# P4's accumulating loads issued behind P7's, and parked slabs moved in pieces, in a two-layer encoder trunk

## The chip, the cores and the metric

The kernel runs on one core of one Trainium2 chip. The metric is the device time of one execution in microseconds (us); lower is better. Three executions of the kernel before gave 1471.56, 1477.7 and 1478.32 us, median 1477.7 us.

## The reference

Two layers of one mixer over 512 positions of width 2048, all in float32, batch 1. Each layer normalises, projects once to all parts, runs three head groups side by side, gates, projects back, normalises and adds to the residual:

```python
for l in range(DEPTH):                       # DEPTH = 2
    h = rmsnorm(x, pre_norm_g[l])
    z = h @ w_in[l]                          # one combined projection
    q_lat, kv_lat, k_pe, gb, gc, xin, q_mem, gate = split_cols(z)
    ...                                      # group A: latent attention, 8 heads, rotary key
    a_out = mla_attention(q, k, v)           # softmax over all 512 positions
    c_out = short_gated_conv(gb, gc, xin, conv_w[l])               # group B: gb * conv3(gc * xin)
    m_out = memory_attention(q_mem, rmsnorm(mem, ...), w_mk[l], w_mv[l])   # group C: 256 memory tokens
    y = jnp.concatenate([a_out, c_out, m_out], axis=-1) * jax.nn.silu(gate)
    x = x + rmsnorm(y @ w_o[l], post_norm_g[l])
```

## The kernel before

**Products.** A float32 product is made of three matmuls on parts with few mantissa bits (`fp32r`): each operand is a high half and a low half, and TensorE adds high x high, high x low and low x high (L272 to L274). The weights' halves are made on the chip from a loaded tile `wr`: ScalarE casts it to `wh` (L189), and VectorE subtracts `wh` from `wr` to get `wl` (L190). This is done two units ahead of TensorE, in pools of three buffers; raw tiles are loaded some six units further ahead, in a pool of eight.

**Groups.** The input projection is cut into groups of two blocks of 512 columns each (416 in group gs[2]). A group is computed with seven products P1 to P7 in place of eight, in Winograd's form of Strassen's scheme, whose right operands are sums of the four weight blocks B11, B12, B21, B22. Each product has four parts c = 0..3, and one part is one step: 12 matmuls on TensorE. The output projection is cut in the same way.

**Where the sums of weights come from.** In a group of the kind `STEADY` (gs[2], gs[3] and gs[4] of each layer, six in all) the order of products is P1; P5 and P2 by turns; P6 and P3 by turns; P7; P4. One tile T per part c begins as B11 for P1. For P5, VectorE adds B12 to it, and for P6, B22 (L178), both loaded by SP. For P4, B21 is added by the transfer itself: a load with `accum_op` add, issued by POOL (the function `more`, L146). P3 uses B22 as loaded; P7 uses the same tile after an accumulating load of B12, also from POOL. An accumulating load can be issued only when the halves of the tile's use before have been made: P4's part c after P6's, P7's part c after P3's. As P6 and P3 go by turns, so do P4's and P7's loads in POOL's queue, though TensorE needs all of P7 before any of P4. A unit's `behind` holds its accumulating load back until the unit it names has been prepared: in groups of the kind `SECOND` (most of the output projection) parts 2 and 3 of P4 wait so for P7's last part.

**Parked slabs.** Results of the projection that are needed in another layout (gc and gb of the convolution, query latents ql, key and value latents kvl, the memory queries qm, the gates gm, ga0, ga1) are written by POOL to DRAM (`sent`, L945: one transfer of 1 MB, kvl in two) and later fetched back into a slab in SBUF with the positions in another order (`fetched`, L952: four transfers of 256 KB, by b = 0..3). A list of calls between the steps says where: gc and gb are written at steps 7 and 8 of gs[2] and fetched at step 3 of gs[3], ql and kvl written at step 21 of gs[3] and fetched at step 2 of gs[4] (tiles cqL, ckvL), qm and gm written at steps 5 and 6 of gs[4], qm fetched at step 10 (QmL), gm at step 23. Then come Km, the rotary table `tab` and Vm, which are read in the mixer behind the group.

**Order.** TensorE, POOL and SP run their instructions in the order in which the code writes them. Beyond the opening part of the kernel VectorE and ScalarE run in an order that a scheduler chose at build time. POOL's transfers complete on eight lanes in turn, and one waits until the transfer eight before it has landed.

Of the kernel before, what the change touches and what calls it, by code (L numbers as in the profile page):

```python
# [5 lines left out]
F32 = mybir.dt.float32  # L6
# [6 lines left out]
P = 128  # L13
D = 2048
# [213 lines left out]
def encoder(tc, x, xt, mem, memt, positions, columns, w_in, q_norm_g, w_uq, w_qr, kv_norm_g, w_ukv,  # L228
# [22 lines left out]
    G = {}  # L251
# [245 lines left out]
    def group(left, key, w, block, slot, passes, final, hold=None, by_two=False, direct=None):  # L497
# [25 lines left out]
        def unit(q, c):  # L523
            k = lambda n: (key, n, c)

            def of(name, loads=(), more=None, sums=(), then=(), **kw):
                at = {"B11": (0, 0), "B12": (0, 1), "B21": (1, 0), "B22": (1, 1)}
                return Unit(k(name), {k(to): [block(*at[n], c)] for to, n in loads}, more and block(*at[more], c),
                            [(k(a), k(b)) for a, b in sums], [(k(a), k(b)) for a, b in then], **kw)
# [5 lines left out]
            if q == "P4":  # L535
                return of("T", more="B21", alloc=hold, behind=(key, "B22", 3) if passes is SECOND and c > 1 else None)
# [401 lines left out]
    def sent(key, *parts):  # L938

        n = sum(t.shape[-1] for t in parts) // 4  # L940
        d = G["sent", key] = dram.tile([4, P, n], F32, name=nm(f"sent{key}"))
        o = 0
        for t in parts:
            w = t.shape[-1] // 4
            nc.gpsimd.dma_start(d[:, :, o:o + w].rearrange("b q k -> q b k"), t.rearrange("q (b k) -> q b k", b=4))  # L945
            o += w

    def fetched(key, name, c=4):

        t, d = slab(name), G.pop(("sent", key))  # L950
        for b in range(4):
            nc.gpsimd.dma_start(t[32 * b:32 * b + 32, :512 * c].rearrange("i (p k) -> i p k", p=4),  # L952
                              d[b].rearrange("(p i) k -> i p k", p=4))
        return t

    def sent_rows(name, C):
        def f():
            pr.until(lambda: C.get((name, "turned")) == NT)
            sent(name, C[name, "slab"])
        return f  # L960

    def gate_back(k, name):
        def f():
            G["ys"][k] = spots(fetched(name, "y"))
        return f

    def conv_back():
        G["uw"] = fetched("gc", "u")
        G["ys"][2] = spots(fetched("gb", "y"))
# [65 lines left out]
    def latents_sent(l):  # L1035
        pr.until(lambda: G.get("normalised") == l)
        sent("ql", G.pop("ql"))
        kv = G.pop("kvl")
        sent("kvl", kv[:, :1024], kv[:, 1024:1536])

    def latents_back():
        G["cqw"], G["ckw"] = fetched("ql", "cqL"), fetched("kvl", "ckvL", 3)
# [242 lines left out]
    def mixer(l, C, pair2, tail):  # L1285
# [5 lines left out]
        add(sent_rows("ga1", C))  # L1291
# [10 lines left out]
        between.setdefault(2, []).append((sent_rows("ga0", C), []))  # L1302
        between.setdefault(11, []).append((gate_back(0, "ga0"), []))
# [3 lines left out]
        between.setdefault(18, []).append((gate_back(1, "ga1"), []))  # L1307
# [165 lines left out]

    def weave(steps, extra, every, n=1):

        out, extra = [], list(extra)
        for k, s in enumerate(steps):
            out.append(s)
            if (k + 1) % every == 0:
                out += extra[:n]  # L1480
                extra = extra[n:]
        return out + extra
# [10 lines left out]
    for l in range(depth):  # L1493
# [109 lines left out]
        put(*gs[l > 0][2:])  # L1603
        add(owns[2])
        steps = [s for passes in gs[2] for s in passes]
        put(steps[:7])
        add(sent_rows(("gb", "gc")[l], C))
        put(steps[7:8])
        add(sent_rows(("gc", "gb")[l], C))
        if l == 0:  # L1610
            add(tables)
        put(steps[8:])
        add(owns[3])
        add(lambda l=l: latents_rows(l))
        steps = [s for passes in gs[3] for s in passes]
        put(steps[:2])
        add(lambda l=l, C=C: latents_begin(l, C))
        put(steps[2:3])
        add(conv_back)
        put(steps[3:8])  # L1620
        add(lambda l=l, C=C: k_rope(l, C))
        put(steps[8:18])
        add(lambda l=l: pr.until(lambda: G.get("normalised") == l))
        put(steps[18:21])
        add(lambda l=l: latents_sent(l))
        put(steps[21:22])
        add(conv(l, 0))
        put(steps[22:25])
        add(conv(l, 1))
        put(steps[25:])  # L1630
        add(owns[4])
        g4 = [s for steps in gs[4] for s in steps]
        put(g4[:1])
        add(conv(l, 2))
        put(g4[1:2])
        add(latents_back)
        put(g4[2:3])
        add(conv(l, 3))
        put(g4[3:5])
        add(sent_rows("qm", C))  # L1640
        put(g4[5:6])
        add(sent_rows("gm", C))
        if l == 0:
            add(tables_wide)
        put(g4[6:7])
        add(latents_parts)
        put(g4[7:9])
        if l == 0:
            add(tables_turned)
        put(g4[9:10])  # L1650
        add(lambda: G.update(qmw=fetched("qm", "QmL")))
        put(g4[10:20])
        add(qm_parts)
        put(g4[20:23])
        add(gate_back(3, "gm"))
        put(g4[23:26])
        add(mem_fetch("Km", 4))
        put(g4[26:27])
        add(tables_fetch)
        put(g4[27:])  # L1660
# [92 lines left out]
```

## Time and profile before

| what | value |
|---|---|
| median of three executions | 1477.7 us (1471.56 to 1478.32) |
| the profiled execution | 1476.04 us, its span 1474.3 us |
| TensorE (PE) busy | 1442.1 us, 98% of the span |
| VectorE (DVE) / ScalarE (ACT) / GpSimd (POOL) busy | 1138.1 / 868.7 / 288.6 us |
| mean granted TensorE clock | 0.994 |
| moved by POOL's queue (q0, software) / SP's (q1, hardware) | 146.03 MB / 162.35 MB |
| accumulating loads of `w_in`, 512 KB: issue to landing | 92, median 7.3 us |
| plain loads of `w_in`, 512 KB, by SP: issue to landing | 128, median 5.8 us |

The profile is of one execution. Times inside it count from the start of the span. A row of waits names the engine and line that waited, for whom, and the total, the count and the longest in us. A row of the timeline gives start and length in us, engine, line, operation, the tile written and the tile read, and in brackets how long the engine stood idle before and who released it. A row of transfers gives what is written and read, the issuing engine, how many, the size of each and the median time from issue to landing. In a row of a group of instructions the busy time and the mean length of one (ns) stand behind the first bar. The "clock" is the share of TensorE's full clock that was granted.

### The profile page before, as it was taken

The numbers are of one execution on the slowest core, as the hardware profiler recorded it, in microseconds if no ns is written. First come the engines' busy times: TensorE is split into PE (matmuls) and PEld (weight loads), VectorE is DVE, ScalarE is ACT, GpSimd is POOL, SyncE is SP. The second block draws the span as 40 slices with busy tenths as digits, with TensorE's granted clock in tenths as the row PEclk, the third lists the DMA queues.
The fourth block names the chain that finished last, engine by engine and source line by source line (L and its number), as shares of the span: only waits on it lengthen the run. The fifth ranks groups of instructions, "written<-read, shape, count | busy, mean of one in ns | idle before, by whom it ended". The sixth has DMA issues, their size and how long they took to land.

```text
span 1474.3 us, 19214 instructions
## 1 busy us (share of the span) xinstructions
PE 1442.1 (98%) x6944; PEld 1223.7 (83%) x6944; DVE 1138.1 (77%) x1517; ACT 868.7 (59%) x1330; POOL 288.6 (20%) x330
## 2 busy tenths in 40 slices
PE   9999999999899999999999999999989999999997
PEld 8887889887688888888898888898867888888886
DVE  5899688696667789769788765768957787688687
ACT  7856344564457788754687433446554586786443
POOL 0032302232132010220220233022322120003111
PEclk9999999999999999999999999999999999999999
DMA  9999977789599194595987999788997984138973
GB/s 358 404 273 211 222 218 143 209 181 314 147 253 265 52 266 133 111 193 172 340 304 224 235 211 226 225 170 219 192 296 162 313 213 97 47 86 151 262 173 128
DMA packets 145567, 309.61 MB, mean 210 GB/s; under 512 B 11008, under 2 KB 32000, under 8 KB 141632
## 3 DMA queue, kind: packets, MB, share of 16 engines
q0 software_dynamic: 58720, 146.03, 45.5%
q1 hardware_dynamic: 86752, 162.35, 34.5%
q8 instruction: 54, 0.88, 0.3%
q14 instruction: 41, 0.34, 0.1%
HBM read 270.47 MB, written 37.88 MB: 209 GB/s over the span
## 4 chain that ended last, share of the span: by engine, by line
PE 71%; DMA 10%; DVE 8%; issue 8%; ACT 2%; POOL 1%; POOLq 0%; SPq 0%; DVEq 0%; ACTq 0%
PE P L273 16%; PE P L274 16%; PE P L272 15%; DMA wr<-in_w_in_dram 7%; DVE wl L190 4%; PE ptp L1219 2%; PE o L273 1%; PE o L274 1%; PE o L272 1%; PE sc L274 1%; PE sc L273 1%; PE sc L272 1%; ACT wh L189 1%; PE qps L272 1%; POOL wr L146 1%
## 5 line engine op out<-in xcount | busy, mean ns | idle before, releaser
L189 ACT CAST wh<-wr 128x1024 fp32r<-128x1024 f32 (+2 forms) x436 | 443.7, 1023 | 437.2 <-PE P L274 306.4
L190 DVE TENSOR_TENSOR wl<-wr,wh 128x1024 fp32r<-128x1024 f32 (+2 forms) x436 | 513.2, 1183 | 198.0 <-ACT wh L189 195.0
L273 PE MATMUL P<-wl,S 128*128 128x512 f32 (+1 forms) x896 | 345.9, 386 | 9.7 <-DVE wl L190 9.5
L272 PE MATMUL P<-wh,S 128*128 128x512 f32 (+1 forms) x896 | 344.9, 385 | 1.9 <-ACT wh L189 1.9
L274 PE MATMUL P<-wh,S 128*128 128x512 f32 (+1 forms) x896 | 344.3, 384 | 0.0
L273 PE MATMUL P<-wl,A 128*128 128x512 f32 (+1 forms) x656 | 253.9, 387 | 10.3 <-DVE wl L190 10.3
L272 PE MATMUL P<-wh,A 128*128 128x512 f32 (+1 forms) x656 | 253.5, 386 | 0.0
L274 PE MATMUL P<-wh,A 128*128 128x512 f32 (+1 forms) x656 | 252.3, 385 | 0.0
L273 PEld LDWEIGHTS P<-wl,S 128*128 128x128 f32 x896 | 168.8, 188 | 43.3 <-DVE wl L190 13.2
L272 PEld LDWEIGHTS P<-wh,S 128*128 128x128 f32 x896 | 168.6, 188 | 32.6 <-ACT wh L189 2.2
L274 PEld LDWEIGHTS P<-wh,S 128*128 128x128 f32 x896 | 168.9, 189 | 30.2
L146 POOL DMA_DIRECT2D wr<-in_w_in_dram x108 | 130.8, 1211 | 305.5 <-DVE wl L190 194.4
L273 PEld LDWEIGHTS P<-wl,A 128*128 128x128 f32 x656 | 123.8, 189 | 36.3 <-DVE wl L190 14.7
L272 PEld LDWEIGHTS P<-wh,A 128*128 128x128 f32 x656 | 123.8, 189 | 22.1 <-ACT og L592 0.2
L274 PEld LDWEIGHTS P<-wh,A 128*128 128x128 f32 x656 | 123.7, 189 | 22.0
L146 POOL DMA_DIRECT2D wr<-in_w_o_dram x40 | 48.8, 1295 | 298.7 <-DVE wl L190 292.8
L178 DVE TENSOR_TENSOR wr<-wr,wr 128x1024 f32<-128x1024 f32 (+1 forms) x60 | 70.0, 1168 | 44.4 <-DMA wr<-in_w_in_dram 43.8
L1206 ACT ACTIVATE P<-sc,nm 128x512 f32<-128x512 f32 (+1 forms) x96 | 59.9, 625 | 28.8 <-DVE nm L1203 28.8
L1209 ACT ACTIVATE P<-P,rec 128x512 f32<-128x512 f32 (+1 forms) x96 | 62.6, 663 | 6.2 <-DVE rec L1208 6.2
L1203 DVE TENSOR_REDUCE nm<-sc 128x1 f32<-128x512 f32 (+1 forms) x96 | 56.4, 594 | 9.1 <-PE sc L1201 8.0
L1219 PE MATMUL ptp<-identr,P 128*128 128x128 f32 x320 | 46.1, 272 | 0.3 <-ACT P L1209 0.3
L1219 PEld LDWEIGHTS ptp<-identr,P 128*128 128x128 f32 x320 | 38.2, 140 | 6.5 <-ACT P L1209 0.7
(325 smaller groups left out, 2102.3 us busy)
## 6 DMA issues: line engine op xcount, KB each, us to landing
wr<-in_w_in_dram SPq DMA_DIRECT2D x128, 512.0 KB, 5.8
wr<-in_w_in_dram POOLq DMA_DIRECT2D x92, 512.0 KB, 7.3
wr<-in_w_o_dram SPq DMA_DIRECT2D x48, 512.0 KB, 6.8
wr<-in_w_o_dram POOLq DMA_DIRECT2D x40, 512.0 KB, 6.7
wr<-in_w_in_dram SPq DMA_DIRECT2D x32, 416.0 KB, 3.9
wr<-in_w_mk_dram SPq DMA_DIRECT2D x15, 512.0 KB, 8.7
wr<-in_w_mv_dram SPq DMA_DIRECT2D x15, 512.0 KB, 10.6
wr<-in_w_in_dram POOLq DMA_DIRECT2D x16, 416.0 KB, 6.7
```

The source lines that it names most:

```text
L146: engine.dma_start(dst, src, **kw)
L178: nc.vector.tensor_tensor(tiles[a], tiles[a], tiles[b], op=ALU.add)
L189: pin(nc.scalar.copy(hi[:, h], src[:, h]))
L190: pin(nc.vector.tensor_tensor(lo[:, h], src[:, h], hi[:, h].bitcast(F32), op=ALU.subtract))
L272: nc.tensor.matmul(ps, ah, bh, start=first, stop=False, **kw)
L273: nc.tensor.matmul(ps, ah, bl, start=False, stop=False, **kw)
L274: nc.tensor.matmul(ps, al, bh, start=False, stop=last, **kw)
L1203: nc.vector.tensor_reduce(nmax, ps, axis=AX.X, op=ALU.max, negate=True)
L1206: nc.scalar.activation(pt, ps, AF.Exp, bias=nmax, accum_out=tot)
L1209: nc.scalar.activation(pt, pt, AF.Copy, scale=rec)
L1219: nc.tensor.transpose(ps[:, k * P:(k + 1) * P], pt[:, k * P:(k + 1) * P], G["ident"])
```

## The change

In `STEADY` groups P4's part c now waits behind a use of B22's part (c + 3) mod 4: part 0 behind P3's part 3, parts 1 to 3 behind P7's parts 0 to 2. And `sent` and `fetched` return lists of four pieces of 256 KB each (kvl is still written in two), which a new function `beside_steps` puts one by one ahead of consecutive steps. New places: in gs[2] steps 4 to 7 and 8 to 11 for the convolution's rows; in gs[3] steps 0 to 3 and 4 to 7 for their fetches and 20 to 25 for ql and kvl; in gs[4] steps 0 to 7 for the latents' fetch (their split moves from step 6 to 9), 4 to 7 and 8 to 11 for qm and gm, 18 to 21 for the fetch of QmL (10 before; its split from 20 to 22) and 23 to 26 for gm's. In the mixer ga1 is written in four pieces at once, ga0 in four pieces between places 2 and 5, and both are fetched piece by piece from 10 and 18 on.

```diff
             if q == "P4":
-                return of("T", more="B21", alloc=hold, behind=(key, "B22", 3) if passes is SECOND and c > 1 else None)
+                return of("T", more="B21", alloc=hold, behind=(key, "B22", 3) if passes is SECOND and c > 1 else
+                          (key, "B22", (c + 3) % 4) if passes is STEADY else None)
...
-    def sent(key, *parts):
-
-        n = sum(t.shape[-1] for t in parts) // 4
-        d = G["sent", key] = dram.tile([4, P, n], F32, name=nm(f"sent{key}"))
-        o = 0
-        for t in parts:
-            w = t.shape[-1] // 4
-            nc.gpsimd.dma_start(d[:, :, o:o + w].rearrange("b q k -> q b k"), t.rearrange("q (b k) -> q b k", b=4))
-            o += w
-
-    def fetched(key, name, c=4):
-
-        t, d = slab(name), G.pop(("sent", key))
-        for b in range(4):
-            nc.gpsimd.dma_start(t[32 * b:32 * b + 32, :512 * c].rearrange("i (p k) -> i p k", p=4),
-                              d[b].rearrange("(p i) k -> i p k", p=4))
-        return t
+    def sent(key, source, *widths):
+
+        def piece(n, b):
+            def f():
+                t, o = source(), sum(widths[:n])
+                if (n, b) in ((0, 0), (0, None)):
+                    G["sent", key] = dram.tile([4, P, sum(widths) // 4], F32, name=nm(f"sent{key}"))
+                w = widths[n] // 4
+                d, t = G["sent", key][:, :, o // 4:o // 4 + w], t[:, o:o + widths[n]].rearrange("q (b k) -> q b k", b=4)
+                if b is None:
+                    nc.gpsimd.dma_start(d.rearrange("b q k -> q b k"), t)
+                else:
+                    nc.gpsimd.dma_start(d[b], t[:, b])
+            return f
+        if len(widths) > 1:
+            return [piece(n, None) for n in range(len(widths))]
+        return [piece(0, b) for b in range(4)]
+
+    def fetched(key, name, there, c=4):
+
+        def piece(b):
+            def f():
+                if b == 0:
+                    G["back", key] = slab(name)
+                t, d = G["back", key], G["sent", key]
+                nc.gpsimd.dma_start(t[32 * b:32 * b + 32, :512 * c].rearrange("i (p k) -> i p k", p=4),
+                                    d[b].rearrange("(p i) k -> i p k", p=4))
+                if b == 3:
+                    there(G.pop(("back", key)))
+            return f
+        return [piece(b) for b in range(4)]
...
-        between.setdefault(2, []).append((sent_rows("ga0", C), []))
-        between.setdefault(11, []).append((gate_back(0, "ga0"), []))
+        for k, f in zip((2, 3, 4, 5), rows_sent("ga0", C)):
+            between.setdefault(k, []).append((f, []))
+        for k, f in zip((10, 11, 12, 13), y_back(0, "ga0")):
+            between.setdefault(k, []).append((f, []))
...
+    def beside_steps(steps, extra):
+        at = {}
+        for first, fs in extra:
+            for k, f in enumerate(fs):
+                at.setdefault(first + k, []).append(f)
+        for k in range(max([len(steps)] + [n + 1 for n in at])):
+            for f in at.get(k, ()):
+                add(f)
+            put(steps[k:k + 1])
...
-        put(steps[:2])
-        add(lambda l=l, C=C: latents_begin(l, C))
-        put(steps[2:3])
-        add(conv_back)
...
-        put(steps[18:21])
-        add(lambda l=l: latents_sent(l))
...
+        beside_steps([s for passes in gs[3] for s in passes],
+                     [(0, fetched("gc", "u", kept_as("uw"))), (2, [lambda l=l, C=C: latents_begin(l, C)]),
+                      (4, y_back(2, "gb")), (8, [lambda l=l, C=C: k_rope(l, C)]),
+                      (18, [lambda l=l: pr.until(lambda: G.get("normalised") == l)]),
+                      (20, latents_sent(l)), (21, [conv(l, 0)]), (25, [conv(l, 1)])])
...
-        put(g4[9:10])
-        add(lambda: G.update(qmw=fetched("qm", "QmL")))
-        put(g4[10:20])
-        add(qm_parts)
...
+        beside_steps([s for passes in gs[4] for s in passes],
+                     [(0, latents_back()), (1, [conv(l, 2)]), (3, [conv(l, 3)]), (4, rows_sent("qm", C)), (6, wide),
+                      (8, rows_sent("gm", C)), (8, turned), (9, [latents_parts]), (18, fetched("qm", "QmL", kept_as("qmw"))),
+                      (22, [qm_parts]), (23, y_back(3, "gm")), (26, [mem_fetch("Km", 4)]), (27, [tables_fetch])])
```

How POOL's queue moves is seen in three places of layer 0. In these rows `wr_` with its number is a weight tile, and each row an accumulating load into it or a transfer to or from a parked slab; the line of the fetch is L952 before and L964 now, of the write L945 before and L949 or L951 now.

The end of gs[2], before (tiles 1682, 1702, 1720 and 1738 are T's parts 0 to 3, loaded for P4; the others are P7's):

```order
L146 DMA wr_1682<-in_w_in_dram 128x2x416
L146 DMA wr_1917<-in_w_in_dram 128x2x416
L146 DMA wr_1702<-in_w_in_dram 128x2x416
L146 DMA wr_1956<-in_w_in_dram 128x2x416
L146 DMA wr_1720<-in_w_in_dram 128x2x416
L146 DMA wr_2010<-in_w_in_dram 128x2x416
L146 DMA wr_1738<-in_w_in_dram 128x2x416
L146 DMA wr_2051<-in_w_in_dram 128x2x416
```

And now:

```order
L146 DMA wr_1919<-in_w_in_dram 128x2x416
L146 DMA wr_1960<-in_w_in_dram 128x2x416
L146 DMA wr_1998<-in_w_in_dram 128x2x416
L146 DMA wr_2056<-in_w_in_dram 128x2x416
L146 DMA wr_1682<-in_w_in_dram 128x2x416
L146 DMA wr_1702<-in_w_in_dram 128x2x416
L146 DMA wr_1720<-in_w_in_dram 128x2x416
L146 DMA wr_1738<-in_w_in_dram 128x2x416
```

P7's four parts now stand in a row, and P4's behind them.

The seam of gs[3] and gs[4], before (2275 to 2329 are P4's tiles):

```order
L146 DMA wr_2329<-in_w_in_dram 128x2x512
L146 DMA wr_2676<-in_w_in_dram 128x2x512
L945 DMA sentql_2884<-ql_2469 128x4x512
L945 DMA sentkvl_2886<-kvl_2470 128x4x256
L945 DMA sentkvl_2886<-kvl_2470 128x4x128
L952 DMA cqL_3088<-sentql_2884 32x4x512 x4
L952 DMA ckvL_3093<-sentkvl_2886 32x4x384 x4
L945 DMA sentqm_3165<-qm_2426 128x4x512
```

And now:

```order
L146 DMA wr_2682<-in_w_in_dram 128x2x512
L146 DMA wr_2280<-in_w_in_dram 128x2x512
L146 DMA wr_2299<-in_w_in_dram 128x2x512
L146 DMA wr_2317<-in_w_in_dram 128x2x512
L951 DMA sentql_2871<-ql_2479 128x512
L146 DMA wr_2335<-in_w_in_dram 128x2x512
L951 DMA sentql_2871<-ql_2479 128x512 x3
L949 DMA sentkvl_2962<-kvl_2480 128x4x256
L949 DMA sentkvl_2962<-kvl_2480 128x4x128
L964 DMA cqL_3052<-sentql_2871 32x4x512 x4
L964 DMA ckvL_3148<-sentkvl_2962 32x4x384
L951 DMA sentqm_3150<-qm_2432 128x512
```

P4's four loads stand behind P7's (the first row is P7's part 3), one piece of ql between them and the other pieces behind; the fetch of ckvL (row by row) is mixed with the pieces of qm.

The end of gs[4], before (2866 to 2932 are P4's tiles; QmL's four pieces are one row):

```order
L952 DMA QmL_3288<-sentqm_3165 32x4x512 x4
L146 DMA wr_2866<-in_w_in_dram 128x2x512
L146 DMA wr_3144<-in_w_in_dram 128x2x512
L146 DMA wr_2889<-in_w_in_dram 128x2x512
L146 DMA wr_3191<-in_w_in_dram 128x2x512
L146 DMA wr_2914<-in_w_in_dram 128x2x512
L146 DMA wr_3234<-in_w_in_dram 128x2x512
L146 DMA wr_2932<-in_w_in_dram 128x2x512
L146 DMA wr_3293<-in_w_in_dram 128x2x512
L952 DMA y_3545<-sentgm_3185 32x4x512 x4
```

And now (P4's tiles are 2873 to 2938):

```order
L146 DMA wr_3300<-in_w_in_dram 128x2x512
L146 DMA wr_2873<-in_w_in_dram 128x2x512
L964 DMA QmL_3452<-sentqm_3150 32x4x512
L146 DMA wr_2900<-in_w_in_dram 128x2x512
L964 DMA QmL_3452<-sentqm_3150 32x4x512
L146 DMA wr_2919<-in_w_in_dram 128x2x512
L964 DMA QmL_3452<-sentqm_3150 32x4x512
L146 DMA wr_2938<-in_w_in_dram 128x2x512
L964 DMA QmL_3452<-sentqm_3150 32x4x512
L964 DMA y_3560<-sentgm_3236 32x4x512 x4
```

QmL's fetch has moved from ahead of all eight loads to between P4's four.

More of the change, by code (lines that the diff above doesn't have):

```diff
@@ L956, in sent_rows @@
-    def sent_rows(name, C):
-        def f():
-            pr.until(lambda: C.get((name, "turned")) == NT)
[L959 to L969, printed above, removed]
+    def sent(key, source, *widths):
[14 more added lines that the diff above has]
+        return [piece(0, b) for b in range(4)]
@@ L971, in conv, with rows_sent, source, kept_as @@
+    def rows_sent(name, C):
+        def source():
+            pr.until(lambda: C.get((name, "turned")) == NT)
+            return C[name, "slab"]
+        return sent(name, source, D)
+    def kept_as(name):
+        return lambda t: G.update({name: t})
+    def y_back(k, name):
+        return fetched(name, "y", lambda t: G["ys"].update({k: spots(t)}))
     def conv(l, c):
@@ L1035, in latents_sent, with source, f @@
     def latents_sent(l):
[L1036 to L1039, printed above, removed]
+        def source(name):
+            def f():
+                pr.until(lambda: G.get("normalised") == l)
+                return G[name]
+            return f
+        return sent("ql", source("ql"), D) + sent("kvl", source("kvl"), 1024, 512)
     def latents_back():
-        G["cqw"], G["ckw"] = fetched("ql", "cqL"), fetched("kvl", "ckvL", 3)
+        return fetched("ql", "cqL", kept_as("cqw")) + fetched("kvl", "ckvL", kept_as("ckw"), 3)
     def latents_parts():
@@ L1290, in mixer @@
         put(p0[1:])
-        add(sent_rows("ga1", C))
+        for f in rows_sent("ga1", C):
+            add(f)
         add(lambda: nc.scalar.activation(small(1, "ex"), C["ga0"][:, NT - 1][:, 0, :1], AF.Exp, scale=0.0))
@@ L1306, in mixer @@
         between.setdefault(7, []).append((fetch0, []))
-        between.setdefault(18, []).append((gate_back(1, "ga1"), []))
+        for k, f in zip((18, 19, 20, 21), y_back(1, "ga1")):
+            between.setdefault(k, []).append((f, []))
         between[m - 2] = [(lambda: pr.prep_next(), [])]
@@ L1472, in put @@
                 add(*s)
+    def beside_steps(steps, extra):
[5 more added lines that the diff above has]
+            for f in at.get(k, ()):
+                add(f)
+            put(steps[k:k + 1])
     def weave(steps, extra, every, n=1):
@@ L1603, in encoder @@
         put(*gs[l > 0][2:])
+        wide, turned = ([tables_wide], [tables_turned]) if l == 0 else ([], [])
+        conv_rows = [rows_sent(n, C) for n in (("gb", "gc") if l == 0 else ("gc", "gb"))]
         add(owns[2])
[L1605 to L1612, printed above, removed]
+        beside_steps([s for passes in gs[2] for s in passes],
+                     [(4, conv_rows[0]), (8, conv_rows[1]), (9, [tables] * (l == 0))])
@@ L1613, in encoder @@
         add(owns[3])
         add(lambda l=l: latents_rows(l))
-        steps = [s for passes in gs[3] for s in passes]
-        put(steps[:2])
-        add(lambda l=l, C=C: latents_begin(l, C))
-        put(steps[2:3])
-        add(conv_back)
[L1620 to L1623, printed above, removed]
-        put(steps[18:21])
-        add(lambda l=l: latents_sent(l))
-        put(steps[21:22])
@@ L1627, in encoder @@
[L1627 to L1630, printed above, removed]
-        add(owns[4])
[L1632 to L1649, printed above, removed]
-        put(g4[9:10])
-        add(lambda: G.update(qmw=fetched("qm", "QmL")))
-        put(g4[10:20])
-        add(qm_parts)
[L1654 to L1660, printed above, removed]
+        beside_steps([s for passes in gs[3] for s in passes],
[3 more added lines that the diff above has]
+                      (20, latents_sent(l)), (21, [conv(l, 0)]), (25, [conv(l, 1)])])
```

## The prediction

> **What bounds the kernel now.** I read the page's busy times first, then TensorE's waits, then the stretches in which it waits, and then the DMA queues there.
>
> ```profile
> span 1474.3 us, 19214 instructions
> PE 1442.1 (98%) x6944; PEld 1223.7 (83%) x6944; DVE 1138.1 (77%) x1517; ACT 868.7 (59%) x1330; POOL 288.6 (20%) x330
> q0 software_dynamic: 58720, 146.03, 45.5%
> q1 hardware_dynamic: 86752, 162.35, 34.5%
> PE P L273 <- DVE wl L190: 19.8, 13, 5.7
> PE P L272 <- ACT wh L189: 1.9, 1, 1.9
> ```
>
> TensorE is busy for 98% of the span, and the change takes no matmul away. So only its waits can be won: 19.8 us in 13 waits for the low halves and 1.9 us for a high half, beside what the clock loses after a wait. The high and low halves are made from weight tiles, so the question is which transfers come late. Windows over the worst places (their columns: stretch, length, then busy time of PE, PEld, DVE, ACT and POOL with counts, granted clock, DMA share, GB/s):
>
> ```profile
> 263.00:270.00 7.00, 5.67 (x20) 5.21 (x21) 4.62 (x6) 4.05 (x6) 0.00 (x0) 0.76 0.61 202
> 355.00:375.00 20.00, 15.33 (x65) 11.74 (x64) 11.77 (x12) 10.89 (x13) 0.76 (x1) 1.00 0.81 268
> 402.00:408.00 6.00, 5.74 (x18) 4.61 (x19) 4.39 (x7) 3.28 (x4) 3.62 (x3) 0.68 0.62 95
> 1094.00:1101.00 7.00, 5.67 (x18) 4.58 (x19) 5.99 (x7) 1.05 (x1) 0.77 (x1) 0.76 0.83 255
> ```
>
> The first is the end of the group gs[2] in layer 0, the second the seam of gs[3] and gs[4], the third the middle of gs[4], and the last the same seam in layer 1. After three of the waits the clock fell; a fallen clock costs length times (1 - clock): 7 x 0.24 = 1.7 us, 6 x 0.32 = 1.9 us and 1.7 us.
>
> **Part 1: P4's accumulating loads go behind P7's.** At the end of gs[2], POOL's timeline, the landing of its last accumulating load (P7's part 3), and TensorE:
>
> ```profile
> 250.65 1.18 POOL L146 DMA_DIRECT2D wr<-in_w_in_dram  x1 [2.07 <-DVE wl L190]
> 252.78 1.21 POOL L146 DMA_DIRECT2D wr<-in_w_in_dram  x1 [0.95 <-DVE wl L190]
> wr<-in_w_in_dram POOLq DMA_DIRECT2D x1, 416.0 KB, 9.9
> 263.73 0.45 PE L272 MATMUL P<-wh,S 128*128 128x416 f32 x1 [1.90 <-ACT wh L189]
> 264.79 0.46 PE L273 MATMUL P<-wl,S 128*128 128x416 f32 x1 [0.61 <-DVE wl L190]
> ```
>
> P4's part 3 (250.65) stands one place ahead of P7's part 3 (252.78) in POOL's queue, though TensorE wants it four steps later. P7's took 9.9 us to land, and TensorE lost 1.90 + 0.61 us and the clock's 1.7. Behind the change nothing of P4 stands ahead: **-4.2 us**. Other short waits (19.8 less 0.6 here and less 5.7, 4.7 and 4.2 named below, 4.6 us) have several causes; I credit 1.5.
>
> What is late next is P4 itself. Its four loads now have no subtraction left to wait for and are issued in a row behind P7's part 3, at a time X. Prices of such a row: alone, in the middle of gs[4], and beside loads from SP, in the output projection, where three are issued together (median landing of the three, and of the last two):
>
> ```profile
> 408.00:418.00 10.00, 10.00 (x46) 8.28 (x45) 4.77 (x4) 3.55 (x4) 4.04 (x4) 1.00 1.11 198
> 640.00:668.00 28.00, 28.00 (x125) 23.17 (x125) 17.84 (x20) 14.92 (x21) 4.92 (x4) 1.00 0.94 228
> 648.19 3.72 POOL L146 DMA_DIRECT2D wr<-in_w_o_dram  x3 [4.23 <-DVE wl L190]
> wr<-in_w_o_dram POOLq DMA_DIRECT2D x1, 512.0 KB, 6.0
> wr<-in_w_o_dram POOLq DMA_DIRECT2D x3, 512.0 KB, 9.7
> wr<-in_w_o_dram POOLq DMA_DIRECT2D x2, 512.0 KB, 11.4
> L189 ACT CAST wh<-wr 128x1024 fp32r<-128x1024 f32 (+2 forms) x436 | 443.7, 1023 | 437.2 <-PE P L274 306.4
> L190 DVE TENSOR_TENSOR wl<-wr,wh 128x1024 fp32r<-128x1024 f32 (+2 forms) x436 | 513.2, 1183 | 198.0 <-ACT wh L189 195.0
> ```
>
> Alone they saturate the engines (share 1.11) at 198 GB/s: 0.524 MB take 2.65 us each. Beside SP's loads the landings are 6.0, 9.7 and 2 x 11.4 - 9.7 = 13.1 us after their own issues, which lie 0.7 us apart or so: X + 6.0, 10.4, 14.5, thus 4.1 us each. A step is 12 matmuls of 28.00/125 = 0.224 us, 2.7 us. Halves are prepared two steps ahead, so P7 begins at X + 5.4 and P4's part k at X + 16.2 + 2.7k; less 2.2 us for the cast and the subtraction (1.02 + 1.18) they must land by X + 14.0, 16.7, 19.4 and 22.1. Alone they land at 8.7, 11.3, 14.0 and 16.6: 5 us early. Beside loads: 10.4, 14.5, 18.6 and 22.7: the last 0.6 late. That gives
> - gs[2], width 416 (loads and steps both 416/512 as long, but not the 2.2 us of preparation nor the first 6.0): 0 to 2 us late, I take **+1.0** per layer, nearer the contended row, since SP is loading the next group;
> - gs[3]: one written piece of the query latents stands ahead of P4's part 3 (256 KB, half of an accumulating load's 2.65 to 4.1 us, so 1.3 to 2.1): 0 to 2.7 late, I take **+1.5**;
> - gs[4]: part 2 below.
>
> On the clock, the row of 263 shows a fall after 2.5 us of waits, while the following longer wait cost no clock (the window 355:375 stands at 1.00):
>
> ```profile
> PE P L273 <- DVE wl L190: 4.7, 3, 3.3
> ```
>
> [...]
>
> **Part 2: pieces, and the fetch of QmL moved from step 10 to steps 18 to 21 of gs[4].** TensorE's longest wait, what VectorE waited for in it, POOL's queue, and the landings of what was issued between 388 and 391:
>
> ```profile
> PE P L273 <- DVE wl L190: 5.7, 1, 5.7
> DVE wr L178 <- DMA wr<-in_w_in_dram: 8.8, 1, 8.8
> 387.78 2.24 POOL L952 DMA_DIRECT2D QmL<-sentqm  x4
> 390.91 1.25 POOL L146 DMA_DIRECT2D wr<-in_w_in_dram  x1 [0.90 <-DVE wl L190]
> QmL<-sentqm POOLq DMA_DIRECT2D x4, 256.0 KB, 7.1
> wr<-in_w_in_dram SPq DMA_DIRECT2D x1, 512.0 KB, 9.7
> ```
>
> VectorE stood 8.8 us before a sum (L178) whose B22 tile took 9.7 us on SP's queue while QmL's four pieces came in; the subtraction TensorE wanted was queued behind that sum on VectorE. With QmL elsewhere the wait and its clock go: 5.7 + 1.9 = **-7.6 us**, in layer 0 only.
>
> QmL now stands between P4's loads: P7's part 3, P4's part 0, QmL, part 1, QmL, part 2, QmL, part 3. Three pieces of 256 KB ahead of part 3, at half of an accumulating load's 2.65 to 4.1 us, add 4.0 to 6.2 us: part 3 lands at 16.6 + 4.0 = 20.6 (in time) to 22.7 + 6.2 = 28.9 (6.8 late). I take **+4.0** per layer with what the clock costs, nearer the upper end, since SP's loads for the query projections run in the same stretch. Behind them come y, Km and the rotary table, pushed back by QmL's four pieces and P4's three loads, some 12 us of queue. Nothing of the trace shows their slack directly, so from 0 (their readers stand in the mixer, beyond P4) to 2 us; I take **+1** per layer.
>
> The remaining waits are at the seam of gs[3] and gs[4]: 4.7 us in layer 0, and in layer 1
>
> ```profile
> PE P L273 <- DVE wl L190: 4.2, 1, 4.2
> DVE wr L178 <- DMA wr<-in_w_in_dram: 7.6, 2, 7.2
> wr<-in_w_in_dram SPq DMA_DIRECT2D x1, 512.0 KB, 14.3
> ckvL<-sentkvl POOLq DMA_DIRECT2D x4, 192.0 KB, 11.5
> ```
>
> with 1.7 us of clock: 10.6 us together. SP's load of 512 KB takes 14.3 us beside the fetched latents. The change helps here by holding ckvL: its first piece must now wait until the last reader of its slab, P1's part 1 of gs[4], is through. It harms by bringing three of P4's loads (8 us alone) into the same stretch. From 0 to all 10.6 could go, or 3 us be added; I take half, **-5.3**. The other pieces cost POOL a little issue time (268 rows become 295, at 2.24/4 = 0.56 us a piece 15 us on an engine that is 20% busy) and move no more bytes; POOL has nothing to wait for between many of them, so they leave as bursts again. I count 0, between -1 and +2 (pieces ahead of an accumulating load).
>
> Sum against the profiled execution's own 1476.04 us: -4.2 - 1.5 - 7.6 - 5.3 = -18.6, and 2 x (1.0 + 1.5 + 4.0 + 1.0) = +15.0; net -3.6, **1472.4 us**. It lies 1.6 us under the median of the runs shown (1477.7); I say **1472**.
>
> **The rivals.**
> - *P4 becomes the wait everywhere* (slower). The place is the four queued loads, and it decides as soon as each takes over (22.1 - 6.0)/4 = 4.0 us; the contended row reads 4.1. With every new cost at its upper end (2 + 2.7 + 6.8 + 2 per layer, 27 us) and the seams unchanged, since P4's loads fill them, the gains of 4.2 + 1.5 + 7.6 leave +13.7: 1490. [...] For it: shares of 0.94 and 1.11 in the rows above. Against it: no wait of TensorE is listed around 648, where two of P4's stand behind P7's. [...]
> - *Nothing changes* because the seams stay as they are (the same bytes in a saturated stretch, P4's moved into it): 1476.0 - 13.3 + 15 = 1478.
> - *Every wait goes*: the 21.7 us listed and 5.3 of clock, less 8 for the lower half of the new costs: 1457.
> - *The pieces do not spread*, so that part 2 is only the moved QmL: that is in my sum already, and costs it nothing.
>
> **How the numbers follow.** My forecast 0.42 (its own spread 1464 to 1480: the seams' 5.3 either way, and some 3 of the other terms), P4 the new wait 0.21, every wait gone 0.20, nothing changes 0.17. The range, 1458 to 1487, reaches nearly to the figures of both sides; outside lie half of the slower rival and less than half of the case with every wait gone, 2 in 10. A measurement of this kernel tells 0.5% from no change: below 1470.3 is faster, above 1485.1 slower, against 1477.7. Faster: 0.19 of my forecast, all 0.20 of the waits gone, 0.01 of no change: 0.40. Slower: 0.17 of the slower rival, 0.02 and 0.03 of my forecast and of no change: 0.22. The same: what is left, 0.38.
>
> **What would show it.** In the changed profile the waits at 262 and 396 are gone and the windows there have a clock of 1.00; TensorE's listed waits are fewer than 21.7 us in all, and the longest stand at P4's parts 2 and 3 of gs[4], with QmL landing between. If the seam at 359 still shows 3 us or more, half of the gain I took there is wrong. If P4 waits in gs[2] and gs[3] too by over 2 us, the first rival holds; if no P4 waits at all, the lone price of 2.65 us was the right one.

## The result: slower by 2.6%, and the profile after

The changed kernel takes 1512.81 us (median of four, 1511.45 to 1515.34) against 1474.69 us before: a ratio of 1.026, 95% interval 1.0225 to 1.0294. The forecast, 1472 us and between 1458 and 1487, was wrong, on the wrong side. The profiled execution took 1511.88 us.

The page of the changed kernel, and what TensorE waited for in it:

```profile
span 1510.1 us, 19221 instructions
PE 1449.4 (96%) x6944; PEld 1227.0 (81%) x6944; DVE 1136.7 (75%) x1517; ACT 868.5 (58%) x1330; POOL 309.8 (21%) x372
PE P L273 <- DVE wl L190: 20.1, 15, 4.7
PE ptp L1233 <- ACT P L1223: 17.6, 8, 6.8
PE P L272 <- ACT qm L593: 5.7, 2, 3.9
PE P L272 <- ACT lat L593: 3.7, 2, 2.2
```

The span grew by 35.8 us. The waits for low halves are as many as before (20.1 us against 19.8), but three rows are new: 17.6 us at `ptp` (L1233), the transposes behind the first softmax of the mixer, and 9.4 us for `qm` and `lat` (L593), the copies of P7's product out of its bank.

Each kernel of this study runs 6944 matmuls in the same order (only eight small ones that turn the rotary table, in layer 0, stand one step earlier where the slabs move in pieces, inside one stretch), so the start of the same matmul can be compared. The table gives how much longer (+) or shorter (-) each stretch was than in the kernel before, in us, layer 0 / layer 1, worked out from these starts; a wait counts to the stretch of the matmul that waited:

| stretch | changed | P4's order alone | pieces alone | pieces, QmL at 10 |
|---|---|---|---|---|
| P7 and P4 of gs[2] | -0.6 / +3.0 | -1.0 / +2.6 | -1.9 / 0.0 | +1.2 / +1.7 |
| gs[3], P1 to P7 | +1.9 / +3.5 | +0.2 / +0.3 | 0.0 / +0.7 | -0.2 / +0.8 |
| P4 of gs[3] | +4.4 / +6.7 | +4.0 / +6.2 | 0.0 / 0.0 | 0.0 / 0.0 |
| gs[4], P1 to P3 | -5.7 / -1.7 | -1.5 / +3.1 | -13.5 / -1.8 | -13.5 / -6.8 |
| P7 and P4 of gs[4] | +2.0 / +1.7 | 0.0 / -0.6 | +3.0 / +0.5 | +0.9 / +1.3 |
| head of the mixer | +11.3 / +11.0 | +8.9 / +8.3 | +2.6 / +2.6 | 0.0 / 0.0 |

The table is of one execution each, and for P4's order alone it was 5 us faster than the median (1503.45 us). In a single stretch the executions differ by up to 3 us where the kernels are alike: the last two columns differ only in gs[4], and read -1.9 and +1.2 in the first row.

**The head of the mixer**, 22 of the 36 us. What TensorE waited for there in layer 0, its row, ScalarE's and VectorE's rows before it, two windows (columns as in the prediction), the SP load of w_uq issued at 426.8, and the two queues between 443.8 and 458.2 (packets, MB, share of the 16 engines), all of the changed kernel:

```profile
PE ptp L1233 <- ACT P L1223: 6.6, 2, 6.3
463.62 0.69 PE L1233 MATMUL ptp<-identr,P 128*128 128x128 f32 x2 [6.32 <-ACT P L1223]
458.59 1.04 ACT L189 CAST wh<-wr 128x1024 fp32r<-128x1024 f32 x1 [10.47 <-DMA wr<-in_w_uq_dram]
459.67 1.23 DVE L190 TENSOR_TENSOR wl<-wr,wh 128x1024 fp32r<-128x1024 f32 x1 [10.67 <-ACT wh L189]
461.41 0.42 DVE L1217 TENSOR_REDUCE nm<-sc 128x1 f32<-128x256 f32 x1
459.40:463.60 4.20, 0.00 (x0) 0.00 (x0) 3.93 (x7) 1.82 (x6) 0.00 (x0) 0.50 1.05 351
463.60:469.60 6.00, 5.22 (x16) 3.82 (x16) 6.00 (x15) 4.37 (x12) 1.70 (x3) 0.50 0.30 114
wr<-in_w_uq_dram SPq DMA_DIRECT2D x1, 256.0 KB, 31.7
q0 software_dynamic: 968, 4.34, 81.4%
q1 hardware_dynamic: 1214, 1.01, 24.3%
```

ScalarE stood 10.47 us before the cast of a tile of w_uq, and VectorE 10.67 us before the subtraction of the same tile. The softmax of the mixer's first heads was queued behind both: its exponentials on ScalarE, and the row maximum that they need (`nm`, L1217) on VectorE. TensorE waited 6.6 us for it. The clock stood at 0.50 from 459.4 to 469.6; while TensorE waited, until 463.6, that cost nothing, and over the 6.0 us behind it some 3.0 us. The second half of the tile took 31.7 us to land. In the 14.4 us before it landed, POOL's queue moved 4.34 MB and SP's 1.01. In the kernel before, the same pair of loads, issued at 430.3 and 430.7, and the two queues between 434 and 441:

```profile
wr<-in_w_uq_dram SPq DMA_DIRECT2D x2, 256.0 KB, 8.8
q1 hardware_dynamic: 2440, 2.42, 108.4%
q0 software_dynamic: 4, 0.02, 0.6%
```

There the loads landed in 8.8 us: from 434 to 441, while they landed, POOL's queue had next to nothing to move (0.02 MB), and SP's queue, with 2.42 MB, had the engines to itself.

**P4's first matmul.** ScalarE and TensorE at the end of gs[2], layer 0, of the changed kernel, and the landing of P4's part 1, whose issue began at 250.5:

```profile
wr<-in_w_in_dram POOLq DMA_DIRECT2D x1, 416.0 KB, 12.5
259.46 0.89 ACT L189 CAST wh<-wr 128x832 fp32r<-128x832 f32 x1 [3.13 <-DMA wr<-in_w_in_dram]
263.02 0.88 ACT L189 CAST wh<-wr 128x832 fp32r<-128x832 f32 x1 [2.68 <-DMA wr<-in_w_in_dram]
263.82 0.91 ACT L593 COPY lat<-P 128x416 f32<-128x416 f32 x2
264.37 0.46 PE L272 MATMUL P<-wh,A 128*128 128x416 f32 x1 [2.17 <-ACT lat L593]
```

In these groups P4 goes on in the banks in which P1 and P7 were summed (`onto` in the code), and P7's result must be copied out of them first (L593). On ScalarE that copy stands behind the cast of P4's part 1 (263.02). That part landed late (250.5 + 12.5 = 263.0), the copy started late, and P4's part 0, whose own cast had begun at 259.46, waited 2.17 us.

### The profile page after: what moved, and what is told of

The parts are those of the page before. It is cut to its first block, busy times and chain, and to the rows that moved or that the text cites. A ratio compares the mean times of both kernels' runs of the same rounds, so it can differ in the third digit from the quotient of the medians.

```text
span 1510.1 us, 19221 instructions
## 1 busy us (share of the span) xinstructions
PE 1449.4 (96%) x6944; PEld 1227.0 (81%) x6944; DVE 1136.7 (75%) x1517; ACT 868.5 (58%) x1330; POOL 309.8 (21%) x372
## 4 chain that ended last, share of the span: by engine, by line
PE 57%; DMA 18%; DVE 10%; issue 8%; POOL 3%; ACT 3%; SPq 0%; POOLq 0%; DVEq 0%; ACTq 0%
DMA wr<-in_w_in_dram 12%; PE P L273 12%; PE P L274 12%; PE P L272 12%; DVE wl L190 5%; DMA wr<-in_w_uq_dram 4%; POOL wr L146 3%; PE ptp L1233 2%; ACT wh L189 1%; PE o L273 1%; PE o L274 1%; PE o L272 1%; PE sc L274 1%; PE sc L272 1%; PE sc L273 1%
## 5 line engine op out<-in xcount | busy, mean ns | idle before, releaser
L272 PE MATMUL P<-wh,S 128*128 128x512 f32 (+1 forms) x896 | 343.8, 384 | 0.0
L272 PE MATMUL P<-wh,A 128*128 128x512 f32 (+1 forms) x656 | 255.8, 390 | 11.4 <-ACT qm L593 5.7
L272 PEld LDWEIGHTS P<-wh,S 128*128 128x128 f32 x896 | 168.1, 188 | 30.1
L272 PEld LDWEIGHTS P<-wh,A 128*128 128x128 f32 x656 | 124.6, 190 | 37.5 <-ACT qm L593 6.6
L1233 PE MATMUL ptp<-identr,P 128*128 128x128 f32 x320 | 47.4, 277 | 17.6 <-ACT P L1223 17.6
L1217 DVE TENSOR_REDUCE nm<-sc 128x1 f32<-128x512 f32 (+1 forms) x96 | 56.8, 595 | 6.4 <-PE sc L1215 6.0
L1233 PEld LDWEIGHTS ptp<-identr,P 128*128 128x128 f32 x320 | 38.3, 142 | 25.7 <-ACT P L1223 20.1
## 6 DMA issues: line engine op xcount, KB each, us to landing
wr<-in_w_mv_dram SPq DMA_DIRECT2D x15, 512.0 KB, 10.6
```

The costliest lines, as they stand in the source:

```text
L272: nc.tensor.matmul(ps, ah, bh, start=first, stop=False, **kw)
L1217: nc.vector.tensor_reduce(nmax, ps, axis=AX.X, op=ALU.max, negate=True)
L1233: nc.tensor.transpose(ps[:, k * P:(k + 1) * P], pt[:, k * P:(k + 1) * P], G["ident"])
```

## The experiments

Theory A, formed on the two traces, held QmL's late fetch and P4's late loads together responsible, as one backlog; theory B the order of P4's loads alone; theory C the pieces.

**P4's order alone.**

```diff
# the kernel before
-  return of("T", more="B21", alloc=hold, behind=(key, "B22", 3) if passes is SECOND and c > 1 else None)
+  return of("T", more="B21", alloc=hold, behind=(key, "B22", 3) if passes is SECOND and c > 1 else
+            (key, "B22", (c + 3) % 4) if passes is STEADY else None)
```

> The kernel before with the first part alone: P4's accumulating loads behind P7's in the steady groups; slabs still move in single calls and QmL is fetched at step 10. Theory A (the loss at the head of the mixer, about 11 us a layer, comes of the backlog that QmL's late fetch and P4's late loads together leave on the transfer engines, which starves SP's loads of w_uq): without QmL in the tail the head of the mixer waits 0 to 4 us a layer; the end of gs[2] gains some 3 us, gs[3] and its seam lose some 5 a layer; 1478 to 1490 us. Theory B (the order of P4's loads is the whole loss, by late parts that hold up ScalarE's queue): about 1505 to 1512 us. Theory C (the pieces are the loss): 1468 to 1477 us.

1508.79 us, ratio 1.0229 (1.0206 to 1.0253). Nearly the whole loss (35 of 38 us), inside B's numbers and outside A's. Its waits:

```profile
PE P L273 <- DVE wl L190: 17.4, 9, 6.1
PE ptp L1220 <- ACT P L1210: 11.7, 2, 6.2
PE P L272 <- ACT qm L593: 6.2, 2, 4.3
PE P L272 <- ACT lat L593: 3.9, 2, 2.5
ACT wh L189 <- DMA wr<-in_w_uq_dram: 18.2, 3, 8.7
```

Both new kinds of wait are there without a single piece and with QmL fetched at step 10: the head of the mixer does not need QmL in its tail.

**The pieces alone** (the changed kernel with this line back):

```diff
# the changed kernel
-                          (key, "B22", (c + 3) % 4) if passes is STEADY else None)
+                          None)
```

> The changed kernel with P4's loads back to taking turns with P7's; pieces and their places as changed, QmL fetched behind all eight loads. Theory A: P4's loads are early again and only QmL's 1 MB is added to the tail: the head of the mixer waits 0 to 6 us a layer, the 5.7 us wait in the middle of gs[4] is gone; 1468 to 1485 us. Theory B: 1466 to 1475 us. Theory C: 1500 to 1512 us.

1466.55 us, ratio 0.9953 (0.9936 to 0.9969): a little faster, inside B's range and 1.5 us below A's. C falls.

```profile
PE P L273 <- DVE wl L190: 5.3, 5, 3.2
PE ptp L1232 <- ACT P L1222: 5.2, 4, 1.5
PE P L272 <- ACT ga L592: 2.5, 2, 1.6
```

The low halves cost 5.3 us in place of 19.8; both the seam and the middle of gs[4] of layer 0 are won (-13.5 us). No cast waits for w_uq. New are 5.2 us at the head of the mixer and 2.5 us at P4's start in gs[4].

**QmL's fetch back to steps 10 to 13 in the changed kernel.**

```diff
-  (18, fetched("qm", "QmL", kept_as("qmw"))), (22, [qm_parts]), ...
+  (10, fetched("qm", "QmL", kept_as("qmw"))), (20, [qm_parts]), ...
```

> The changed kernel with the fetch of QmL back at step 10, still as four pieces (steps 10 to 13), and its split back at step 20. Theory A: 1 MB less in the tail of gs[4], about 5.6 us of the engines' time, so the wait at the head of the mixer falls from about 11 to 4 us or less a layer; the wait in the middle of gs[4] of layer 0 may come back with up to 7 us; 1492 to 1505 us. Theory B: P4's loads are as late as before except in gs[4] itself: 1505 to 1513 us. Theory C: 1508 to 1515 us.

1498.87 us, ratio 1.0171 (1.0153 to 1.0188): 14 us better than the changed kernel, inside A's range and outside B's, but the head of the mixer still loses 9.2 and 6.2 us. QmL's late fetch adds to the backlog; it is not what makes it.

**QmL's fetch at step 18 in the kernel before**, as one burst (its split at 22):

> The kernel before with one edit: QmL's fetch as one burst at step 18 of gs[4] (its split at 22). Theory A: the wait of 5.7 us and its clock in layer 0 are gone (-7.6), and 1 MB more in the tail costs 0 to 4 us a layer at the head of the mixer: 1467 to 1476 us. If QmL's late fetch alone makes the loss at the head: 1485 us or more. Theories B and C: 1466 to 1469 us.

```diff
# the kernel before
-        put(g4[9:10])
-        add(lambda: G.update(qmw=fetched("qm", "QmL")))
-        put(g4[10:20])
+        put(g4[9:18])
+        add(lambda: G.update(qmw=fetched("qm", "QmL")))
+        put(g4[18:22])
         add(qm_parts)
```

1475.63 us, ratio 1.0006 (0.9991 to 1.002): no change, at the upper edge of A's range. The wait in the middle of gs[4] of layer 0 is gone (-7.4 us in that stretch) and the gain is given back: +5.3 and +1.6 us at P7 and P4 of gs[4], +2.6 us at the head of the mixer in each layer. The stretch I had booked as -7.6 was right, and the move's price of 1 us too small. Theories B and C, at 1466 to 1469 us, missed.

So neither A nor B held alone. These four left a theory D: P4's late loads cost at places of their own, by two mechanisms: the cast of part 1 ahead of P7's copy on ScalarE, and in gs[4] the backlog that starves SP's loads for the mixer. The next two runs split the change by group.

**P4's order in gs[2] and gs[3] only**, and **in gs[4] only** (otherwise the changed kernel):

```diff
-  (key, "B22", (c + 3) % 4) if passes is STEADY else None)
+  (key, "B22", (c + 3) % 4) if passes is STEADY and key[1] != 4 else None)     # the first of the two
+  (key, "B22", (c + 3) % 4) if passes is STEADY and key[1] == 4 else None)     # the second
```

> The changed kernel with P4's loads behind P7's in gs[2] and gs[3] alone; in gs[4] they take turns with P7's again. Theory D (the four late loads cost at three places of their own: ScalarE casts P4's part 1 ahead of reading P7's product out of the bank that P4 goes on with, so a late part 1 stops TensorE at P4's first matmul; the loads push the seam; and in gs[4] they leave SP's loads for the mixer starved): the wait at the head of the mixer falls from 11 us a layer to the 3 us that it has with the pieces alone, gs[2] and gs[3] stay as in the changed kernel: 1492 to 1499 us. Rival (the head of the mixer waits because of what gs[3] and the seam delayed, or because of the pieces): 1505 to 1513 us.

> The changed kernel with P4's loads behind P7's in gs[4] alone. Theory D: if the three groups cost each on their own, this and the run without gs[4] add up to the changed kernel and the one with the pieces alone: 1480 to 1488 us, with the wait at the head of the mixer as long as in the changed kernel and none at P4's start in gs[2] and gs[3]. Rival (a shared backlog that runs from group to group): 1466 to 1474 us, the head of the mixer as with the pieces alone.

1497.38 us, ratio 1.0155 (1.0126 to 1.0184), and 1485.2 us, ratio 1.0072 (1.0048 to 1.0096): both as theory D had it. Against the pieces alone they cost 30.8 and 18.7 us; the sum, 49.5, stands against 46.3 for the whole change. (The profiled execution of the second took 1492.35 us, 7 more than its median, so its rows are of its slowest execution.) The rows at the head of the mixer, first without and then with gs[4], and what ScalarE waited for in the second:

```profile
PE ptp L1233 <- ACT P L1223: 5.2, 4, 1.5
```

```profile
PE ptp L1233 <- ACT P L1223: 17.4, 8, 6.9
ACT wh L189 <- DMA wr<-in_w_uq_dram: 21.8, 2, 10.9
```

In the first no cast waits for w_uq, and the head of the mixer loses 2.6 us a layer, as with the pieces alone: of P4's loads, those of gs[4] alone decide it. In the first, the waits at P4's start stay (`qm` 5.5 us, `lat` 4.8), and gs[4] up to P3 gains only 5.3 us in layer 0 where the pieces alone, and the second run too, gain 13.5: late loads in the groups before take the rest of the pieces' gain there, most likely those of gs[3], next to it.

**Only parts 2 and 3 of P4 behind P7's last part**, as the output projection has it:

```diff
-  behind=(key, "B22", 3) if passes is SECOND and c > 1 else (key, "B22", (c + 3) % 4) if passes is STEADY else None)
+  behind=(key, "B22", 3) if (passes is SECOND or passes is STEADY) and c > 1 else None)
```

> The changed kernel with only parts 2 and 3 of P4 behind P7's last part, as the output projection has it; parts 0 and 1 take turns with P7's. Theory D: part 1 is early again, so TensorE doesn't wait at P4's first matmul for ScalarE's reading of P7's product (10 us of waits and the clock behind them in the changed kernel); two loads less in each tail, so the head of the mixer waits 3 to 7 us a layer: 1470 to 1485 us. Rival (any of P4's loads behind P7's last part costs what four do): 1500 us or more.

1485.93 us, ratio 1.0069 (1.0049 to 1.009), 1 us above D's range.

```profile
PE P L273 <- DVE wl L190: 17.7, 13, 4.0
PE ptp L1232 <- ACT P L1222: 11.2, 6, 3.9
ACT wh L189 <- DMA wr<-in_w_uq_dram: 19.2, 4, 5.4
```

No row for `qm` or `lat` is left: with part 1 early, P7's copy is not held up, and the stretch P7 and P4 of gs[2] gains 4.6 us in layer 0. This is the first mechanism, shown from its other side. The head of the mixer lies between (+6.2 and +7.9 us, against +11.3 and +11.0 in the changed kernel), with two late loads in place of four.

**The pieces, with QmL's fetch at steps 10 to 13** (the two edits above together):

> The pieces alone (P4's loads take turns with P7's) and QmL's fetch in pieces at steps 10 to 13, its split at 20. Theory D: with 1 MB less in the tail the waits at the head of the mixer (1.7 and 1.4 us) and at P4's start in gs[4] (2.0 and 1.2) are gone in both layers, some 8 us less than the pieces alone, and as pieces QmL does not hold up SP's load in the middle of gs[4]: 1457 to 1464 us. Rival (the wait of 5.7 us in the middle of gs[4] comes back with its clock): 1466 to 1474 us.

1462.77 us, ratio 0.9913 (0.9882 to 0.9944), inside D's range; the interval lies below 1. The head of the mixer costs nothing (0.3 us in the waits), and the middle of gs[4] keeps its gain (-13.5 us in the stretch): with QmL in pieces between the writes of gm, only 0.6 us of waits of TensorE are listed between 355 and 440. Whether that comes of cutting QmL or of the new places of the slabs around it was not taken apart.

**ga1's written pieces (1 MB) from the head of the mixer to its places 6 to 9**, in the changed kernel:

```diff
-        for f in rows_sent("ga1", C):
-            add(f)
...
+        for k, f in zip((6, 7, 8, 9), rows_sent("ga1", C)):
+            between.setdefault(k, []).append((f, []))
```

> The changed kernel with the four written pieces of ga1 (1 MB) moved from the head of the mixer to its places 6 to 9, behind the loads that SP has in flight there. Theory D (the head of the mixer waits for SP's load of w_uq, which shares the engines with POOL's backlog): 1 MB less ahead of it, at some 400 GB/s 2.6 us, so the wait for w_uq on ScalarE falls from 10.5 and 10.9 us to 7 to 9 in each layer: 1504 to 1510 us. Rival (the head waits for Km, the table or QmL, which stand ahead of ga1 in POOL's queue): the same wait, 1511 to 1515 us.

1521.02 us, ratio 1.0301 (1.0269 to 1.0332): a miss in the time, a hit in the wait.

```profile
PE ptp L1233 <- ACT P L1223: 12.8, 8, 4.7
PE o L272 <- ACT PT L277: 4.8, 2, 2.4
ACT wh L189 <- DMA wr<-in_w_uq_dram: 8.4, 1, 8.4
457.56 1.04 ACT L189 CAST wh<-wr 128x1024 fp32r<-128x1024 f32 x1 [8.90 <-PE qps L274]
```

In layer 1 the cast waits 8.4 us for w_uq, not 10.9; in layer 0 the same cast stands still for 8.90 us, not 10.47 (the row names TensorE, which had come last by a little), and TensorE's wait falls from 17.6 to 12.8 us. So what POOL's queue moves while SP's load is under way does set this wait (in the changed kernel ga1's pieces were issued from 443.5 on, with w_uq still to land at 458.5). The stretch as a whole gains less, 0.1 us in layer 0 and 1 in layer 1, and more than that is lost behind it: 5.2 and 3.3 us more than in the changed kernel in the stretches behind the two heads, of which 4.8 are new waits of the mixer (L272, two of them), and 3.1 in gs[4] of layer 1. That ga1's later 1 MB causes them by meeting the fetches of the rotary parts and of ga0 is likely but not shown.

**What was left of the old waits.** With all else won, the kernel with the pieces and QmL at 10 still waits some 4 us at the end of gs[2] of layer 0. Two ways to put P7's last load forward there:

```diff
# the pieces, QmL at 10; P4's parts 2 and 3 behind P7's last part in gs[2] only:
+  behind=(key, "B22", 3) if c > 1 and (passes is SECOND or key[1] == 2) else None)
# or P4's part 3 alone, in all three groups:
+  behind=(key, "B22", 3) if c > 1 and passes is SECOND or c > 2 and passes is STEADY else None)
```

> The pieces, QmL's fetch at steps 10 to 13, and P4's parts 2 and 3 behind P7's last part in gs[2] alone. Theory D: the wait at the end of gs[2] (3.4 + 1.1 us and 1.7 of clock in layer 0, 0.9 + 1.1 in layer 1) is gone and nothing takes its place, since gs[2] has no tail with other transfers behind it: 1453 to 1459 us. Rival (parts 2 and 3 of P4 are late instead, as in the changed kernel): 1462 to 1468 us.

> The pieces, QmL's fetch at steps 10 to 13, and part 3 of P4 alone behind P7's part 3, in all three steady groups (a swap of two neighbours in POOL's queue). Theory D: the swap brings P7's part 3 forward by one load, about 3 us, so most of the wait at the end of gs[2] is gone, and P4's part 3 still lands in time: 1454 to 1461 us, no wait at P4's first matmul. Rival (the head of the mixer waits again for w_uq): 1463 us or more.

1458.32 us, ratio 0.989 (0.9868 to 0.9911), and 1462.8 us, ratio 0.9917 (0.9894 to 0.994). In both the end of gs[2] gains 4.6 us in layer 0 and no wait of TensorE is listed there. In the second the gain is lost in gs[4] up to P3 (-6.2 us in place of -13.5 in layer 0), so the swap in gs[3] or gs[4] undoes there what it wins in gs[2]; that missed D's range by 2 us. The first has the lowest median of the study, 17 us under the kernel before, though its interval overlaps those of the second and of the pieces with QmL at 10 (0.9882 to 0.9944):

```profile
span 1455.7 us, 19263 instructions
PE P L273 <- DVE wl L190: 8.3, 9, 2.6
PE P L272 <- ACT wh L189: 1.1, 2, 0.7
```

## Why the prediction was wrong

- **The waits removed** were right. The end of gs[2] was priced at 4.2 us: with P4 on time it gains 4.6 (the two last runs). The middle of gs[4] was priced at 7.6: QmL's move alone gains 7.4 there. The seam was priced at 5.3 of 10.6; the pieces alone gain 13.5 - 7.4 = 6.1 us in layer 0 and 1.8 in layer 1. In the changed kernel itself the seam of layer 0 still shows a wait of 4.7 us (at 371), which the prediction had named as the sign that half of that gain is wrong.
- **P4 late in gs[4]**, +4.0 a layer: measured +2.0 and +1.7, and the runs give this to QmL's late fetch, not to P4's order. With QmL late and P4's loads early (the pieces alone) the stretch costs +3.0 and +0.5; with P4's loads late and QmL early (P4's order alone, and QmL back at 10 in the changed kernel) 0.0 and -0.6. P7's part 3 was issued at 415.92 (X); P4's part 3 at 426.85 and landed 12.9 us later, at X + 23.8, where I had bounds of 20.6 and 28.9 and a need of 22.1. POOL's rows (the last two) show that the four are not issued in a row, which I had assumed; POOL stood 1.40 and 2.84 us without a releaser that the view names:

```profile
415.92 2.46 POOL L146 DMA_DIRECT2D wr<-in_w_in_dram  x2 [4.35 <-DVE wl L190]
wr<-in_w_in_dram POOLq DMA_DIRECT2D x1, 512.0 KB, 12.9
422.21 1.20 POOL L146 DMA_DIRECT2D wr<-in_w_in_dram  x1 [1.40 <-issue]
426.85 1.23 POOL L146 DMA_DIRECT2D wr<-in_w_in_dram  x1 [2.84 <-issue]
```

The landings tell what it stood for: P7's part 3 landed at 421.90 and P4's part 0 at 426.54, each 0.3 us before the next of these two issues. In this trace none of POOL's 148 accumulating loads begins before the one three places ahead of it has landed, and 51 begin within 0.5 us of that landing. So P4's parts 2 and 3 stood behind those two landings and were not issued at X. What sets this distance of three is not shown. The eight lanes show as well: none of POOL's 340 transfers begins before the one eight places ahead of it has landed, and 24 begin before the one seven places ahead has.

- **P4 late in gs[2] and gs[3]**, +1.0 and +1.5 a layer: measured some +4.0 (-0.6 where -4.6 was to be had) and +3.0 in gs[2], +4.4 and +6.7 in gs[3]. The +3.0 is the least sure: in three profiles with the loads of gs[2] early, that stretch reads 0.0, +1.7 and +3.5. The step that failed is the deadline, "less 2.2 us for the cast and the subtraction": it took each part's need from TensorE's own use of it. Part 1 is needed most of a step earlier, since ScalarE's order puts its cast ahead of the copy that P4's first matmul waits for. The landing times were off by less, 1 to 2 us: in gs[2] of layer 0 P4's parts landed 10.5, 14.1, 17.7 and 21.5 us behind the issue of P7's part 3 (at 248.82), where the contended row, scaled to this width as the prediction says, gives 9.6, 12.9, 16.2 and 19.6. What stood behind the waiting cast on its engine is not shown here.
- **The tail of gs[4]**, +1 a layer: measured +11.3 and +11.0, the largest error, 20 us of the 41 between forecast and result. The step that failed is "Behind them come y, Km and the rotary table": it priced only what stands behind the late loads in POOL's own queue. The victim stood in the other queue: SP's load of w_uq, on the same 16 engines, with the softmax's work on ScalarE and VectorE behind that tile's cast and subtraction. Of the 11 us the pieces alone, with QmL late, make 2.6; P4's late loads of gs[4] make the rest. Smaller, and likely of the same kind: with P4's loads of gs[2] and gs[3] late, gs[4] up to P3 gains 5.3 us in place of the pieces' 13.5, and what waits there is again a sum whose tile SP loads (VectorE's waits of the changed kernel, 355 to 375):

```profile
DVE wr L178 <- DMA wr<-in_w_in_dram: 6.4, 2, 5.6
```

- **The clock.** I counted none for the new waits beyond gs[4]. The head of the mixer in layer 0 alone lost some 3.0 us to it (0.50 over the 6.0 us behind the wait), counted in the row above. That none of them costs clock is a term of the sum that no run shows: in layer 0 of the changed kernel the clock stood at 0.83 around the new wait of 2.17 us at the end of gs[2] (260 to 270), and at 1.00 behind the one of 1.8 us at 344.
- **The rivals.** "P4 becomes the wait everywhere" had the sign, a chance of 0.21 and the figure 1490. It was the right place, but not its only mechanism: P4's own lateness in gs[2] and gs[3] accounts for 15 to 18 us, the mixer for 22. The check that spoke against it, no wait around 648 where two of P4's loads stand behind P7's, was misread: two are not four (parts 0 and 1 were early there), which is just what the run with parts 2 and 3 shows.
- **The pieces do not spread**: partly so, yet the pieces alone are worth 0.5%, and 0.9% with QmL kept early. I had counted them at 0 beyond QmL's move and the seam. POOL's work for them was undercounted: its instructions rose by 42 (330 to 372), not by 27, and its busy time by 21 us, not 15. It stayed busy for 21% of the span.

That the head of the mixer follows POOL's backlog by way of w_uq is shown by four runs (the cast's longest wait for w_uq is 10.9 us with gs[4]'s four late loads alone, 21.8 in all; with two it is 5.4, 19.2 in all; with 1 MB less beside the load it is 8.4 in layer 1; without late loads in gs[4] none is listed). How much of the +1.9 and +3.5 us in gs[3] itself comes from the fetches of u and y was not taken apart.

## What to carry to other kernels

When a transfer is made to wait, list what stands behind it in three places, not one: on its own queue, on the engines that consume it (here a copy and a softmax that had nothing to do with the late tile), and on the other queue that shares the transfer engines. A load's deadline is the earliest of those, and on an engine that runs its instructions in order, as ScalarE did here (the copy at 263.82 behind the cast at 263.02), it can lie well before the first use of its own data. And a part of a change that is good alone can hide behind one that is bad: here, taking them apart turned +2.6% into -1.1%.

## What the runs showed of the hardware

At the head of the mixer, where both queues stayed full, they moved about as many packets each, but not as many bytes, nor in as much of the engines' time: between 443.8 and 458.2 POOL's queue moved 968 packets and SP's 1214, but 4.34 MB against 1.01, in 81.4% and 24.3% of the time. A packet of the first held 4.5 KB on average and one of the second 0.8 (941 of SP's were of 512 bytes, as long as a row of w_uq). In the 17 us before, from the issue of the load on, the counts are all but equal (first two rows, 426.9 to 443.8); the other two are of layer 1, between 1190 and 1207. The counts of a window differ where POOL's queue ran empty before its end: from 443.8 to 455.8 they are 843 and 843, from 455.8 to 458.2 they are 125 and 371, and from 1190 to 1206 they are 1085 and 1088.

```profile
q0 software_dynamic: 1283, 3.18, 83.1%
q1 hardware_dynamic: 1281, 1.02, 26.3%
q0 software_dynamic: 1153, 4.97, 85.1%
q1 hardware_dynamic: 1240, 0.88, 21.7%
```

In bytes, the queue with the small rows got the small share, and 256 KB took 31.7 us. What makes the counts equal is not shown, and the obvious test, w_uq in longer rows, was not tried.

The clock again did not follow the length of a wait. At the end of gs[2] of layer 0 the changed kernel waited 2.17 us and the clock fell (first row, 260 to 270); 80 us later it waited 1.8 us, then 1.0 and 0.8, and it did not fall (second row, 340 to 358); and the pieces alone waited 1.6 + 0.6 us at the same place of gs[2] with a full clock (third row).

```profile
260.00:270.00 10.00, 7.83 (x34) 7.33 (x33) 4.08 (x5) 2.93 (x5) 2.59 (x4) 0.83 1.11 276
340.00:358.00 18.00, 14.46 (x62) 11.10 (x61) 10.25 (x11) 7.30 (x10) 5.02 (x9) 1.00 1.07 325
```

```profile
258.00:268.00 10.00, 7.84 (x41) 7.15 (x40) 5.14 (x7) 5.15 (x7) 0.00 (x0) 1.00 1.03 310
```
